# Every fp32r product reads its moving operand and writes its bank from the last column to the first

## The chip, the cores and the metric

One core of a Trainium2 chip. The metric is the device time of one execution, in microseconds; for the kernel before it is 1514.39 us, the median of three runs (1514.04 to 1516.86).

The engines, as the profile names them: PE multiplies matrices, and PEld loads its stationary operands; DVE and ACT work on vectors; POOL and SP here mostly start transfers. A product on PE holds one operand in the array (the stationary one, 128 x 128) and streams the other through it column by column (the moving one, 128 rows by up to 512 columns). Its result lands in a bank of PSUM, 128 partitions by 512 fp32 columns, column by column.

## The reference

Two layers on a sequence of 512 tokens with 1024 features, all in float32. Layer 0 mixes the tokens by windowed attention in three dilated head groups, layer 1 by a gated linear recurrence; each layer ends with a gated feed-forward net with a short convolution.

```python
for layer in range(DEPTH):
    h = rms_norm(x, norm_mix_pre[layer])
    if layer % 2 == 0:
        h = dilated_attention_mixer(h, attn_w_qkv[j], attn_w_o[j], rel_bias)
    else:
        h = rglru_mixer(h, lru_w_in[j], ...)
    x = x + rms_norm(h, norm_mix_post[layer])
    h = rms_norm(x, norm_ffn_pre[layer])
    h = conv_ffn(h, ffn_w_up[layer], ffn_conv_w[layer], ffn_conv_b[layer], ffn_w_down[layer])
    x = x + rms_norm(h, norm_ffn_post[layer])

def conv_ffn(x, w_up, conv_w, conv_b, w_down):
    u = causal_dwconv(x @ w_up, conv_w, conv_b)
    g, v = u[..., :D_FF], u[..., D_FF:]
    return (jax.nn.gelu(g, approximate=True) * v) @ w_down
```

The weights are what is large: 1024 x 9216 for the queries, keys and values, 1024 x 6144 and 3072 x 1024 for each feed-forward net.

## The kernel before

The program holds the activations of all 512 tokens on the chip and streams the weights through. A plan lists the weight chunks in the order of their use; `load` fetches a chunk with one transfer of 1 MB on SP's queue, and `pump` splits it into two fp32r numbers per weight: a high part (`whi`, ACT, line 146) and what is missing (`wlo`, DVE, line 147). The activations are split in the same way (`hT` is a pair of tiles, `ahi` and `alo` are a pair).

A float32 product is then three fp32r products into the same bank, high by high, high by low and low by high. That is the helper `mm3` (lines 237 to 240), and every large product of the kernel goes through it:

- `feat` (lines 348 to 356): features by tokens. The weights are stationary, the normalized activations `hT` are the moving operand, 8 steps over the 1024 input features. A bank `ps` takes 512 tokens in one go, or two halves of 256 (`feat_tiles` with `halves`, at the start of the recurrence and of each feed-forward net). The bank is evacuated by the sinks: `conv` (line 503 on ACT, line 507 on DVE), `qk` (line 580 on ACT, line 582 on DVE; in the dilated groups with the tokens regrouped, which is a read with a step of four columns).
- `values` (bank `v`): tokens by features for the values of the attention. The activations are stationary, 256 columns of weights move; ACT evacuates at line 614.
- `rows_run` (bank `acc`): the output projections. The split activations are stationary, 512 columns of weights move, and up to eight banks are open at once.
- `gates` (bank `gate`): the two gates of the recurrence.

The other matmuls are plain float32 and call `nc.tensor.matmul` or `transpose` directly: the transposes (`tr` line 289, `PT`, `OT`), the scores (`S`, lines 660 and 710) and the weighted values (`O`, lines 695 and 768). Each of these shows as two rows of the profile.

All matmuls stand on PE in the order in which the program is written. Side steps (attention heads, norms) are generators that `tick` advances between tiles. The eight PSUM banks are used in rotation, and the layer that places the tiles adds the waits on semaphores: `PE_49`, `Activation_49` and `DVE_49` count the instructions that each engine has finished.

Of the kernel before, what the change touches and what calls it, by code (L numbers as in the profile page):

```python
# [76 lines left out]
def kernel(  # L77
# [157 lines left out]
        plan.append(("rows", 2, D, [(w[r0 : r0 + 256, :].rearrange("(k p) c -> p k c", p=P), 2)]))  # L235

    def mm3(dst, l, r, start, stop):
        mm(dst, l[0], r[0], start=start, stop=False)  # L238
        mm(dst, l[0], r[1], start=False, stop=False)  # L239
        mm(dst, l[1], r[0], start=False, stop=stop)  # L240
# [107 lines left out]
    def feat(W, hT, dst, n0, n1):  # L348
        for k in range(KD):
            mm3(  # L350
                dst[:, n0:n1],
                [w[:, k, :] for w in W],
                [h[:, k, n0:n1] for h in hT],
                k == 0,
                k == KD - 1,
            )
# [43 lines left out]
    def rows_run(nchunks, A, prep, seq, order, post, pre):  # L400
# [6 lines left out]
        for tiles, chunks in order:  # L407
            for c in chunks:
# [9 lines left out]
                for n, part in enumerate(loop):  # L418
                    prep(seq.index(2 * c + n) + 3)
                    for t, i, kk in part:  # L420
                        k = 2 * c + kk
                        if t not in banks:
                            banks[t] = [psum("acc"), psum("acc")]
                            left[t] = [2 * nchunks, 2 * nchunks]
                        mm3(
                            banks[t][i],
                            [a[:, t * P : (t + 1) * P] for a in A[k]],
                            [v[:, 0, i * 512 : (i + 1) * 512] for v in take(*W[c][kk])],
                            left[t][i] == 2 * nchunks,
                            left[t][i] == 1,  # L430
                        )
                        left[t][i] -= 1
                        uses[k] -= 1
                        if not uses[k]:
                            done()
                    for t in tiles:
                        if left[t] == [0, 0]:
                            side(norms(t, banks[t], post_g, pre_g, hT))
                    tick()
# [94 lines left out]
    def attention(hT, post, pre):  # L534
# [50 lines left out]
        def values(vs, permute):  # L585
# [10 lines left out]
            for tp in range(2):  # L596
                ps = psum("v")
                for t in (2 * tp, 2 * tp + 1):
                    if first_tiles and t < 2:
                        first_tiles[0](t)  # L600
                    W = W or chunk_pair()
                    tok = slice(t * P, (t + 1) * P)
                    for k in range(KD):
                        mm3(
                            ps[:, (t % 2) * 256 : (t % 2) * 256 + 256],
                            [h[:, k, tok] for h in hT],
                            [v[:, k % 4, :] for v in W[k // 4]],
                            k == 0,
                            k == KD - 1,
                        )  # L610
                if first_tiles and not tp:
                    first_tiles[0](2)
                o = gen(s="v")
                nc.scalar.activation(o, ps, AF.Copy)
                if permute:
                    rows = vd[2 * tp * P : (2 * tp + 2) * P, :]
                    nc.sync.dma_start(rows.rearrange("(t p) c -> p t c", p=P), o.rearrange("p (t c) -> p t c", t=2))
                else:
                    vs.append(o)
                if tp:  # L620
                    done(2)
                    if permute:
                        by_residue(vd, vs)
                tick()
# [384 lines left out]
```

## Time and profile before

| what | value |
|---|---|
| median of three runs | 1514.39 us |
| profiled execution | 1513.89 us |
| its span, first to last instruction | 1512.1 us |
| mean granted TensorE clock | 0.994 |
| PE busy, matmuls | 1482.6 us, 7659 rows |
| weight loads busy (PEld) | 1271.1 us |
| DVE / ACT / POOL busy | 798.5 / 631.5 / 53.5 us |
| HBM | 161 MB, 107 GB/s over the span |

A row of the groups reads: line, engine, operation, output tile <- input tiles, array rows x columns, shape and type, count | busy us, mean ns of one | idle us before them, and what ended it. The type of every tile on PE is printed as f32; the fp32r products are those of lines 238 to 240. Matmuls overlap, so the duration of one (389 ns) is longer than the distance to the next; the distance is read from the starts in the timeline. PEld is the weight load that goes with each matmul, and PEldq or PEq is the queue in front of PE.

### The profile page before, as it was taken

The page shows a single profiled execution, that of the slowest core. Times are in us where ns is not written, and L with a number is a line of the kernel's source. Part 1 is how long each engine was busy: PE and PEld are TensorE (multiplying, and loading weights), DVE is VectorE, ACT ScalarE, POOL GpSimd, SP SyncE. Part 2 cuts the span into 40 slices and gives each one's busy share as a digit, 9 for nine tenths or more (in the row PEclk, how much of TensorE's full clock was granted, in tenths as well). Part 3 has the DMA queues.
Part 4 walks back from the last instruction along what each step waited for, and adds up shares of the span by engine and source line. Part 5 has one row for each costly group of instructions (what it writes and reads, how often), then busy time and mean ns, then how long its engine had stood idle before and what let it go on. Part 6 is the DMA issues. An engine that isn't in the chain of part 4 may idle for free.

```text
span 1512.1 us, 19272 instructions
## 1 busy us (share of the span) xinstructions
PE 1482.6 (98%) x7659; PEld 1271.1 (84%) x7659; DVE 798.5 (53%) x1610; ACT 631.5 (42%) x1281; POOL 53.5 (4%) x81
## 2 busy tenths in 40 slices
PE   6999999999999999999999999999899999999997
PEld 5789989898989898888888888988698888888886
DVE  5344334343434586555555336868776555565333
ACT  5243334343333555344344334477554334344321
POOL 3130000000000000000000000003000000000000
PEclk9999999999999999999999999999999999999999
DMA  6642223333333333323233231252224232323301
GB/s 205 211 155 91 65 94 110 105 121 111 109 121 129 98 112 112 111 84 112 84 111 112 84 112 42 71 166 67 96 80 136 84 111 84 109 86 111 112 1 56
DMA packets 120075, 157.72 MB, mean 104 GB/s; under 512 B 4960, under 2 KB 105528, under 8 KB 119985
## 3 DMA queue, kind: packets, MB, share of 16 engines
q1 hardware_dynamic: 115088, 145.24, 29.1%
q0 software_dynamic: 4896, 11.26, 2.2%
q8 instruction: 60, 0.98, 0.3%
q14 instruction: 31, 0.25, 0.1%
HBM read 150.14 MB, written 11.05 MB: 107 GB/s over the span
## 4 chain that ended last, share of the span: by engine, by line
PE 87%; issue 8%; DVE 3%; DMA 1%; POOL 0%; ACT 0%; SPq 0%; DVEq 0%; POOLq 0%
PE ps L238 17%; PE ps L240 17%; PE ps L239 17%; PE acc L240 7%; PE acc L239 7%; PE acc L238 7%; PE v L238 3%; PE v L240 3%; PE v L239 3%; PE O L768 1%; PE S L710 1%; PE O L695 1%; PE tr L289 1%; DVE wlo L147 1%; DMA toe<-skew 1%
## 5 line engine op out<-in xcount | busy, mean ns | idle before, releaser
L238 PE MATMUL ps<-hT,whi 128*128 128x512 f32 (+1 forms) x1376 | 518.6, 377 | 0.0
L240 PE MATMUL ps<-hT,wlo 128*128 128x512 f32 (+1 forms) x1376 | 515.2, 374 | 0.0
L239 PE MATMUL ps<-hT,whi 128*128 128x512 f32 (+1 forms) x1376 | 515.1, 374 | 0.0
L147 DVE TENSOR_TENSOR wlo<-raw,whi 128x512 fp32r<-128x512 f32 x504 | 324.6, 688 | 284.5 <-ACT whi L146 284.3
L146 ACT ACTIVATE whi<-raw 128x512 fp32r<-128x512 f32 x504 | 285.8, 622 | 132.3 <-PE acc L240 120.9
L240 PEld LDWEIGHTS ps<-hT,wlo 128*128 128x128 f32 x1376 | 259.0, 188 | 46.7
L238 PEld LDWEIGHTS ps<-hT,whi 128*128 128x128 f32 x1376 | 259.1, 188 | 46.3 <-issue 0.6
L239 PEld LDWEIGHTS ps<-hT,whi 128*128 128x128 f32 x1376 | 259.2, 188 | 45.8
L507 DVE SCALAR_TENSOR_TENSOR u<-ps,cols,u 128x511 f32<-128x511 f32 x192 | 143.8, 749 | 140.4 <-ACT u L503 137.0
L240 PE MATMUL acc<-whi,alo 128*128 128x512 f32 x512 | 200.4, 391 | 4.2 <-DVE alo L147 4.2
L238 PE MATMUL acc<-whi,ahi 128*128 128x512 f32 x512 | 200.9, 392 | 1.4 <-ACT ahi L146 1.4
L239 PE MATMUL acc<-wlo,ahi 128*128 128x512 f32 x512 | 200.0, 391 | 0.0
L503 ACT ACTIVATE u<-ps,cols 128x512 f32<-128x512 f32 x96 | 74.8, 779 | 209.8 <-PE ps L240 209.8
L240 PEld LDWEIGHTS acc<-whi,alo 128*128 128x128 f32 x512 | 96.7, 189 | 24.6 <-DVE alo L147 4.7
L238 PEld LDWEIGHTS acc<-whi,ahi 128*128 128x128 f32 x512 | 96.7, 189 | 21.7 <-ACT ahi L146 1.8
L239 PEld LDWEIGHTS acc<-wlo,ahi 128*128 128x128 f32 x512 | 96.6, 189 | 20.0
L238 PE MATMUL v<-whi,hT 128*128 128x256 f32 x384 | 111.9, 291 | 0.4 <-ACT hT L293 0.4
L240 PE MATMUL v<-whi,hT 128*128 128x256 f32 x384 | 110.2, 287 | 0.1
L239 PE MATMUL v<-wlo,hT 128*128 128x256 f32 x384 | 109.8, 286 | 0.0
L238 PEld LDWEIGHTS v<-whi,hT 128*128 128x128 f32 x384 | 75.0, 195 | 1.4 <-ACT hT L293 1.1
L240 PEld LDWEIGHTS v<-whi,hT 128*128 128x128 f32 x384 | 74.7, 195 | 0.7 <-DVE hT L294 0.6
L239 PEld LDWEIGHTS v<-wlo,hT 128*128 128x128 f32 x384 | 75.0, 195 | 0.3
(167 smaller groups left out, 1002.3 us busy)
## 6 DMA issues: line engine op xcount, KB each, us to landing
raw<-in_ffn_w_up_dram SPq DMA_DIRECT2D x48, 1024.0 KB, 5.2
raw<-in_attn_w_qkv_dram SPq DMA_DIRECT2D x36, 1024.0 KB, 5.1
raw<-in_ffn_w_down_dram SPq DMA_DIRECT2D x24, 1024.0 KB, 4.8
raw<-in_lru_w_in_dram SPq DMA_DIRECT2D x8, 1024.0 KB, 5.2
skew<-rowv POOLq DMA_DIRECT2D x3, 1536.0 KB, 12.1
vrows<-v SPq DMA_DIRECT2D x16, 256.0 KB, 3.9
vp<-vrows SPq DMA_DIRECT2D x16, 256.0 KB, 3.0
raw<-in_attn_w_o_dram SPq DMA_DIRECT2D x4, 1024.0 KB, 4.8
```

Source lines behind the costliest of these rows:

```text
L146: nc.scalar.activation(hi, raw, AF.Copy)
L147: nc.vector.tensor_tensor(lo, raw, hi.bitcast(F32), op=ALU.subtract)
L238: mm(dst, l[0], r[0], start=start, stop=False)
L239: mm(dst, l[0], r[1], start=False, stop=False)
L240: mm(dst, l[1], r[0], start=False, stop=stop)
L289: nc.tensor.transpose(ps[:, k * P : (k + 1) * P], xs[i][:, k * P : (k + 1) * P], ident)
L503: nc.scalar.activation(u, ps, AF.Identity, scale=cc[:, j : j + 1], bias=cc[:, 48 + j : 49 + j])
L507: nc.vector.scalar_tensor_tensor(u[:, d:], ps[:, : S - d], wc, u[:, d:], op0=ALU.mult, op1=ALU.add)
L695: mm(po[:, a * P : (a + 1) * P], pts[a, j], vtile(v, a - 1 + j, hh), start=j == js[0], stop=j == 1)
L710: mm(ps[:, c], q[hh][:, c], k[hh][:, c], start=True, stop=True)
L768: mm(po[:, c], vtile(qkvs[gi][2], r, hh), pts[gi][:, c], start=gi == 0, stop=gi == 1)
```

## The change

One line in `mm3`: the view of the bank and the two views of the moving operand are turned around in their second dimension before the three products are issued. The stationary operands stay as they are. Column c of the moving operand still lands in column c of the bank, so what is computed is the same; the stream starts at column 511 (or 255) and ends at 0. The plain float32 matmuls keep their direction.

```diff
     def mm3(dst, l, r, start, stop):
+        dst, r = dst[:, ::-1], [v[:, ::-1] for v in r]
         mm(dst, l[0], r[0], start=start, stop=False)
         mm(dst, l[0], r[1], start=False, stop=False)
         mm(dst, l[1], r[0], start=False, stop=stop)
```

In the built program each engine has the same matmuls, vector instructions and transfers in the same order as before (PE 7428 matmuls in both). What differs beside the direction are waits. On PE, 117 matmuls wait on PE's own count that did not before, and 94 of these waits are waiting instructions of their own. In the program of before, a new bank of the first feed-forward net on PE (bank `ps912`, after the last products of `ps908`):

```order
L240 MATMUL ps908_5589<-hT0733_4547,wlo879_5360 128x512
L238 MATMUL ps912_5625<-hT0733_4547,whi883_5397 128x512 [waits Activation_49]
L239 MATMUL ps912_5625<-hT1734_4548,whi883_5397 128x512
L240 MATMUL ps912_5625<-hT0733_4547,wlo884_5398 128x512 [waits DVE_49]
L238 MATMUL ps912_5625<-hT0733_4547,whi883_5397 128x512
```

The same place on PE in the changed program, whose lines stand one lower:

```order
L241 MATMUL ps908_5589<-hT0733_4547,wlo879_5360 128x512
L239 MATMUL ps912_5625<-hT0733_4547,whi883_5397 128x512 [waits PE_49,Activation_49]
L240 MATMUL ps912_5625<-hT1734_4548,whi883_5397 128x512
L241 MATMUL ps912_5625<-hT0733_4547,wlo884_5398 128x512 [waits DVE_49]
L239 MATMUL ps912_5625<-hT0733_4547,whi883_5397 128x512
```

The first product of the bank waits on `PE_49` as well; the values waited for belong to products 41 to 168 matmuls earlier, over all 117.

On DVE, 93 waits on `PE_49` are gone, and 46 waiting instructions with them. At the split of the weights for that same bank, before:

```order
L507 SCALAR_TENSOR_TENSOR u882_5392<-ps881_5367,cols186_1074,u882_5392 128x511 [waits Activation_49]
L507 SCALAR_TENSOR_TENSOR u882_5392<-ps881_5367,cols186_1074,u882_5392 128x510 [waits DVE_49]
L147 TENSOR_TENSOR wlo884_5398<-raw865_5220,whi883_5397 128x512 [waits DMAHW3_49,PE_49,Activation_49]
L147 TENSOR_TENSOR wlo884_5398<-raw865_5220,whi883_5397 128x512 [waits Activation_49]
L507 SCALAR_TENSOR_TENSOR u886_5428<-ps885_5403,cols186_1074,u886_5428 128x511 [waits Activation_49]
```

And in the changed program:

```order
L508 SCALAR_TENSOR_TENSOR u882_5392<-ps881_5367,cols186_1074,u882_5392 128x511 [waits Activation_49]
L508 SCALAR_TENSOR_TENSOR u882_5392<-ps881_5367,cols186_1074,u882_5392 128x510 [waits DVE_49]
L147 TENSOR_TENSOR wlo884_5398<-raw865_5220,whi883_5397 128x512 [waits DMAHW3_49,Activation_49]
L147 TENSOR_TENSOR wlo884_5398<-raw865_5220,whi883_5397 128x512 [waits Activation_49]
L508 SCALAR_TENSOR_TENSOR u886_5428<-ps885_5403,cols186_1074,u886_5428 128x511 [waits Activation_49]
```

The split still waits for ACT's high half and for the transfer; ACT, POOL and SP hold the same rows and waits as before.

## The prediction

> **What bounds the kernel now.** I read the page first: the shares of busy time, then the chain that ended last.
>
> ```profile
> span 1512.1 us, 19272 instructions
> PE 1482.6 (98%) x7659; PEld 1271.1 (84%) x7659; DVE 798.5 (53%) x1610; ACT 631.5 (42%) x1281; POOL 53.5 (4%) x81
> PEclk9999999999999999999999999999999999999999
> PE 87%; issue 8%; DVE 3%; DMA 1%; POOL 0%; ACT 0%; SPq 0%; DVEq 0%; POOLq 0%
> ```
>
> PE is busy for 1482.6 of 1512.1 us, its granted clock stands in the top tenth in every slice, and 87% of the chain that set the end is PE. PE sits idle for 1512.1 - 1482.6 = 29.5 us in all. So whatever the change does to the time of a matmul comes out at the end, nearly one for one, and whatever it does to another engine does not.
>
> A busy time of pipelined matmuls does not say what one costs, so next I read the timeline of PE, once where the products are 512 columns wide and once where they are 256 wide.
>
> ```profile
> 1375.88 0.39 PE L238 MATMUL acc<-whi,ahi 128*128 128x512 f32 x1
> 1376.10 0.39 PE L239 MATMUL acc<-wlo,ahi 128*128 128x512 f32 x1
> 1376.33 0.39 PE L240 MATMUL acc<-whi,alo 128*128 128x512 f32 x1
> 1376.56 0.39 PE L238 MATMUL acc<-whi,ahi 128*128 128x512 f32 x1
> ```
> ```profile
> 559.91 0.28 PE L238 MATMUL ps<-hT,whi 128*128 128x256 f32 x1
> 560.03 0.28 PE L239 MATMUL ps<-hT,whi 128*128 128x256 f32 x1
> 560.15 0.28 PE L240 MATMUL ps<-hT,wlo 128*128 128x256 f32 x1
> 560.27 0.28 PE L238 MATMUL ps<-hT,whi 128*128 128x256 f32 x1
> ```
>
> The reader is to look at the starts, not the durations. Three products of 512 columns take 1376.56 - 1375.88 = 0.68 us, so one starts every 227 ns. Three of 256 columns take 0.36 us, one every 120 ns. The difference of 107 ns over 256 columns is 0.418 ns a column, and what is left, 120 - 107 = 13 ns, is the same for both widths: a fixed price of each product, in which no column moves.
>
> Then the groups by shape, for how many products there are.
>
> ```profile
> L238 PE MATMUL ps<-hT,whi 128*128 128x512 f32 x1184 | 463.8, 392 | 0.0
> L240 PE MATMUL ps<-hT,wlo 128*128 128x512 f32 x1184 | 461.0, 389 | 0.0
> L239 PE MATMUL ps<-hT,whi 128*128 128x512 f32 x1184 | 460.8, 389 | 0.0
> L238 PE MATMUL acc<-whi,ahi 128*128 128x512 f32 x512 | 200.9, 392 | 1.4 <-ACT ahi L146 1.4
> L240 PE MATMUL acc<-whi,alo 128*128 128x512 f32 x512 | 200.4, 391 | 4.2 <-DVE alo L147 4.2
> L239 PE MATMUL acc<-wlo,ahi 128*128 128x512 f32 x512 | 200.0, 391 | 0.0
> L238 PE MATMUL v<-whi,hT 128*128 128x256 f32 x384 | 111.9, 291 | 0.4 <-ACT hT L293 0.4
> L240 PE MATMUL v<-whi,hT 128*128 128x256 f32 x384 | 110.2, 287 | 0.1
> L239 PE MATMUL v<-wlo,hT 128*128 128x256 f32 x384 | 109.8, 286 | 0.0
> L238 PE MATMUL ps<-hT,whi 128*128 128x256 f32 x192 | 54.8, 285 | 0.0
> L239 PE MATMUL ps<-hT,whi 128*128 128x256 f32 x192 | 54.3, 283 | 0.0
> L240 PE MATMUL ps<-hT,wlo 128*128 128x256 f32 x192 | 54.3, 283 | 0.0
> L238 PE MATMUL gate<-xhi,whi 128*128 128x512 f32 x32 | 12.4, 389 | 0.0
> L239 PE MATMUL gate<-xlo,whi 128*128 128x512 f32 x32 | 12.4, 389 | 0.0
> L240 PE MATMUL gate<-xhi,wlo 128*128 128x512 f32 x32 | 12.4, 389 | 0.0
> ```
>
> These are all the products that `mm3` issues, and all that the change touches. Of 512 columns there are 3 x (1184 + 512 + 32) = 5184, of 256 columns 3 x (384 + 192) = 1728: 6912 products. At 227 and 120 ns that is 1177 + 207 = 1384 us, 92% of the span. In columns it is 5184 x 512 + 1728 x 256 = 3,096,576, and at 0.418 ns each 1294 us is the pure streaming of columns.
>
> **The change, part by part.** It adds and removes no product, changes no shape and moves no instruction. It has two parts with a price: the direction of the streams, and waits.
>
> *The direction.* Each of 6912 products now reads 512 or 256 fp32r columns downward from SBUF, and writes the bank downward. The trace holds no matmul whose operand or output steps by anything but one column upward, so the price is bounded from both sides. The lower end is nothing: the same columns, the same bank, one after the other. Below nothing there is no room that I can name: 0.418 ns a column is the fastest column in this trace, and a direction takes no part in the fixed 13 ns as far as rows show. The upper end comes from the nearest rows in which PE takes its columns slower, the plain f32 products of the attention scores:
>
> ```profile
> L660 PE MATMUL S<-qk,qk 128*128 128x256 f32 x48 | 11.7, 380 | 0.0
> L660 PE MATMUL S<-qk,qk 128*128 128x128 f32 x16 | 3.1, 273 | 0.0
> ```
>
> 128 columns more take 380 - 273 = 107 ns, 0.836 ns a column: twice the price of an fp32r column. fp32r thus takes two columns where these rows take one. If its double rate rests on taking neighbouring columns in rising order as a pair, a falling order loses it, and each column costs 0.836 - 0.418 = 0.418 ns more: 3,096,576 x 0.418 = 1294 us.
>
> Which end is nearer? The trace shows other engines on access patterns with steps. ACT evacuates the score operands' bank at line 580 in plain order before 205 us, and with a step of four columns between 215 and 490 us; line 774 is the one write with a step of four columns, and line 614 is a plain evacuation to set beside it.
>
> ```profile
> L580 ACT ACTIVATE qk<-ps 128x512 f32<-128x512 f32 x10 | 6.0, 596 | 32.4 <-PE ps L240 28.4 <-PE cols L459 4.0
> L580 ACT ACTIVATE qk<-ps 128x512 f32<-128x512 f32 x14 | 8.4, 599 | 59.1 <-PE ps L240 35.5 <-issue 23.6
> L774 ACT ACTIVATE oT<-O 128x512 f32<-128x512 f32 x8 | 8.8, 1097 | 41.8 <-PE O L768 38.3 <-issue 3.5
> L614 ACT ACTIVATE v<-v 128x512 f32<-128x512 f32 x24 | 14.2, 591 | 79.1 <-PE v L240 79.1
> ```
>
> Reading the bank with a step costs ACT nothing (596 against 599 ns); writing SBUF 16 bytes apart costs it 1097 / 591 = 1.86 times. So a pattern's step can double a transfer, but the doubling row is one in which neighbours in time lie 16 bytes apart. Reversed columns lie 4 bytes apart, as near as before, which is the case of the rows without a price. I take nothing as the value, and keep 1294 us as the other end.
>
> Two pages bear on this, and they point in opposite directions. The Trainium skill, "Advanced Engine Details and Errata", section Memory Cachelines, counts how many accesses in a row fall on one line of 16 bytes in SBUF. Line 774 agrees with that (one element a line, 1.86 times), and by that rule a reversed run, four elements a line, stays at 0.418 ns and the time at 1514 us. The Trainium skill, "PSUM — Partial Sum Buffer", section Specifications (TRN2), says that any non-contiguous access pattern slows matmuls significantly. Read strictly, a run with step -1 is such a pattern, and the time would be that of the halved rate below; no row here shows a matmul with such an output.
>
> *The waits.* The changed program asks PE for 117 waits on PE's own earlier products that were not asked before; 94 of them come as a waiting instruction of their own ahead of the matmul (first product of a bank, mostly in the feature tiles of the two FFNs). Behind each stands the whole PE queue. The product waited for lies 41 to 168 products back, at 120 ns or more each at least 41 x 120 ns = 4.9 us, so it has long ended: the wait finds its value there. What is left is the instruction itself. Its kind is in the profile of before:
>
> ```profile
> L238 PEldq EVENT_SEMAPHORE  x41: 51/51/51, 33.6 to 1376.5; - x41
> ```
>
> 51 ns each, if nothing hid it: 94 x 51 ns = 4.8 us, 0.3%. The last of them began at 1376.5, and the timeline quoted above shows the products around it 220 to 230 ns apart, as everywhere: the queue had taken it ahead of time. I take nothing, with 4.8 us as the upper end; if the queue ran dry the cover would be gone.
>
> On DVE 93 waits on PE fall away, at the low halves of the weight splits (line 147). DVE is busy for 53% of the span, and the products waited for line 147 for 4.2 us in the groups above; I take nothing for it, and 4 us of gain at most. POOL, SP and the DMA queues hold the same rows as before.
>
> *Sum.* The profiled execution took 1513.89 us, its span and 1.8 us around it; the median of three runs is 1514.39. With nothing added and nothing taken the forecast is the median, 1514.4 us, and its own range is 1510 (the 4 us from DVE) to 1519 (the 4.8 us of the waits).
>
> **The rivals.** *The falling order loses the double rate* (slower). Its place is every product of `mm3`; it decides as soon as the pairing looks for rising neighbours, on the read or on the write. For it: fp32r is exactly twice as fast as f32 here, which says that something is taken two at a time, and the 1.86 times of line 774. Against it: reversed pairs stay within the same neighbourhood, and the stepped reads of line 580 are free. Price: 1513.9 + 1294 = 2808 us, less at most the 29.5 us of idle time that a slower PE would cover: 2779 to 2808, with line 774's 1.86 in place of 2 it is 1513.9 + 0.86 x 1294 = 2627. I take 2800 us.
>
> *A fixed price per product*: the stream starts at the end of a line, and each product pays something once, between nothing and its present fixed part again, 6912 x 13 ns = 90 us; the exposed 4.8 us of waits are of this kind too. For it: a fixed part exists. Against: it is the same at both widths, so it looks like the change of weights and not like the stream. 1518 to 1604 us.
>
> *A worse loss than the double rate*: each column alone, at twice the f32 price, 4 x 0.418 ns: 1513.9 + 3 x 1294 = 5396 us. No row shows such a rate on PE.
>
> *Faster*: only by the DVE waits that fall away, at most 4 us, 1510. That the two reversals are undone when the program is made into instructions gives the forecast's time.
>
> **How the numbers follow.** The forecast 0.50; the lost double rate 0.32; a fixed price 0.10; the worse loss 0.05; faster 0.03. A measurement of this kernel tells about 0.2%, 3 us, from no change; the forecast stands for "within 0.2%", and the three slower cases together for slower, 0.47. The predicted time is that of the likeliest case. The forecast and the fixed price hold only 0.60, so the range has to reach the lost double rate: 1510 to 2830 us, the last 22 us for a fixed price on top; it leaves out the worse loss and part of the faster case.
>
> **What would show it.** Right: starts of 512-wide products still 227 ns apart and of 256-wide ones 120, durations 389 to 392 and 283 to 291 ns, PE idle near 30 us, the new waits in the rows of PE's queue with the cadence around them unbroken. The lost double rate: starts about 441 and 227 ns apart, so 0.836 ns a column, with the plain f32 rows at 380 and 273 ns as they are, and idle shares of DVE and ACT up. A fixed price: both widths longer by the same number of ns. I am wrong if the starts differ from 227 by more than 1 ns.

## The result, and the profile after

The changed kernel takes 1542.61 us, the median of five runs (1540.88 to 1543.44), against 1514.39 us before: ratio 1.0182, 95% interval 1.0168 to 1.0196, 28 us slower. The forecast was no change. That the time lies in the stated range is luck: the range reached that far for a much larger loss by another mechanism. What happened is nearest to the rival with a fixed price per product, and differs from it in one point that turned out to be the key: the two widths did not change alike.

The page of the changed kernel, the same rows as before:

```profile
span 1540.8 us, 19320 instructions
...
PE 1513.6 (98%) x7659; PEld 1270.4 (82%) x7659; DVE 798.7 (52%) x1610; ACT 631.4 (41%) x1281; POOL 53.2 (3%) x81
...
PEclk9999999999999999999999999999999999999999
...
PE 87%; issue 8%; DVE 3%; DMA 1%; ACT 0%; POOL 0%; DVEq 0%; SPq 0%; POOLq 0%
```

The span grew by 28.7 us; PE's busy time grew by 31.0 us and its idle time shrank by 2.3. No other engine's busy time moved by more than 0.7 us. The clock is as before, and PE's share of the chain that ended last is 87% in both. The 48 instructions more are 94 waits more on PE and 46 fewer on DVE. So the loss lies inside the products, and the timeline shows it in the output projection (512 columns) and in the half banks (256 columns):

```profile
1404.32 0.40 PE L239 MATMUL acc<-whi,ahi 128*128 128x512 f32 x1
1404.55 0.40 PE L240 MATMUL acc<-wlo,ahi 128*128 128x512 f32 x1
1404.79 0.40 PE L241 MATMUL acc<-whi,alo 128*128 128x512 f32 x1
1405.02 0.40 PE L239 MATMUL acc<-whi,ahi 128*128 128x512 f32 x1
...
1405.72 0.40 PE L239 MATMUL acc<-whi,ahi 128*128 128x512 f32 x1
```
```profile
570.06 0.28 PE L239 MATMUL ps<-hT,whi 128*128 128x256 f32 x1
570.18 0.28 PE L240 MATMUL ps<-hT,whi 128*128 128x256 f32 x1
570.30 0.28 PE L241 MATMUL ps<-hT,wlo 128*128 128x256 f32 x1
...
571.48 0.28 PE L239 MATMUL ps<-hT,whi 128*128 128x256 f32 x1
```

Six wide products take 1405.72 - 1404.32 = 1.40 us, 233.3 ns each where it was 226.7. Twelve narrow ones take 571.48 - 570.06 = 1.42 us, 118.3 ns each where it was 120. The wide ones got dearer by 6.7 ns, the narrow ones cheaper by 1.7. The prediction had named starts more than 1 ns off 227 as the sign that it is wrong. The groups by shape show the same for the wide products, which last 8 ns longer (400 and 397 against 392 and 389 ns); a narrow one lasts as long as before, and so does a plain f32 product (`S`, 380 ns), which was not turned around.

```profile
L239 PE MATMUL ps<-hT,whi 128*128 128x512 f32 x1184 | 473.3, 400 | 0.0
L240 PE MATMUL ps<-hT,whi 128*128 128x512 f32 x1184 | 470.5, 397 | 0.0
...
L239 PE MATMUL v<-whi,hT 128*128 128x256 f32 x384 | 111.9, 291 | 0.0
...
L661 PE MATMUL S<-qk,qk 128*128 128x256 f32 x48 | 11.7, 380 | 0.0
```

Summed over the distances between starts in the two traces, the wide products take 31.1 us more (22.4 in `ps`, 8.1 in `acc`, 0.6 in `gate`), the narrow ones 2.2 us less, and everything else 0.1 us less: 28.7 us, the whole difference of the spans.

### The profile page after: what moved, and what is told of

It reads as the page before. It is cut to its first block, busy times and chain, and to the rows that moved or that the text cites. A ratio compares the mean times of both kernels' runs of the same rounds, so it can differ in the third digit from the quotient of the medians.

```text
span 1540.8 us, 19320 instructions
## 1 busy us (share of the span) xinstructions
PE 1513.6 (98%) x7659; PEld 1270.4 (82%) x7659; DVE 798.7 (52%) x1610; ACT 631.4 (41%) x1281; POOL 53.2 (3%) x81
## 4 chain that ended last, share of the span: by engine, by line
PE 87%; issue 8%; DVE 3%; DMA 1%; ACT 0%; POOL 0%; DVEq 0%; SPq 0%; POOLq 0%
PE ps L239 17%; PE ps L241 17%; PE ps L240 17%; PE acc L241 7%; PE acc L240 7%; PE acc L239 7%; PE v L239 3%; PE v L241 3%; PE v L240 3%; PE O L769 1%; PE S L711 1%; PE O L696 1%; PE tr L290 1%; DVE wlo L147 1%; DMA toe<-skew 1%
## 5 line engine op out<-in xcount | busy, mean ns | idle before, releaser
L239 PE MATMUL ps<-hT,whi 128*128 128x512 f32 (+1 forms) x1376 | 527.9, 384 | 0.0
L240 PE MATMUL ps<-hT,whi 128*128 128x512 f32 (+1 forms) x1376 | 524.6, 381 | 0.0
L241 PE MATMUL ps<-hT,wlo 128*128 128x512 f32 (+1 forms) x1376 | 524.5, 381 | 0.0
L241 PE MATMUL acc<-whi,alo 128*128 128x512 f32 x512 | 204.2, 399 | 4.2 <-DVE alo L147 4.2
L239 PE MATMUL acc<-whi,ahi 128*128 128x512 f32 x512 | 204.8, 400 | 0.1
L240 PE MATMUL acc<-wlo,ahi 128*128 128x512 f32 x512 | 204.1, 399 | 0.0
```

## The experiments

Theory one: the downward order of the *read* of the moving operand has a price. Theory two: the downward *write* of the bank has it. Later a third came up: it is not the direction at all, but how the read of the moving operand meets, in SBUF, the load of the next product's weights that runs under it. The waits were the rival from the prediction. Distances of starts given below without a fence are means over the second half of a row of equal products in that run's trace.

### One side alone

```diff
-        dst, r = dst[:, ::-1], [v[:, ::-1] for v in r]
+        r = [v[:, ::-1] for v in r]
```

> Only the moving operand is read downward; the bank is written upward, so every product lands mirrored in its bank (the output is not the reference's). If the price sits in the downward read: 512-wide products start 233 ns apart as in the changed kernel, about 1543 us. If it sits in the downward write: 227 ns and about 1514 us. If it needs both (the two streams against each other): neither, 227 ns and 1514 us. If it were the added waits: 1514 to 1519 us with starts of 227 ns between the waits.

Measured: 1541.62 us, ratio to before 1.0181 (1.0162 to 1.0200).

```diff
-        dst, r = dst[:, ::-1], [v[:, ::-1] for v in r]
+        dst = dst[:, ::-1]
```

> Only the bank is written downward; the moving operand is read upward, so every product lands mirrored (the output is not the reference's). If the price sits in the downward write: 512-wide starts 233 ns apart, about 1543 us. If in the read: 227 ns, about 1514 us. If each direction costs something: e1 and this one between 1514 and 1543 us and adding up to the 28 us.

Measured: 1513.76 us, ratio 0.9998 (0.9989 to 1.0007). The groups of the first and of the second, one row each for the wide products:

```profile
L239 PE MATMUL ps<-hT,whi 128*128 128x512 f32 x1184 | 473.3, 400 | 0.0
```
```profile
L239 PE MATMUL ps<-hT,whi 128*128 128x512 f32 x1184 | 463.8, 392 | 0.0
```

The read carries the whole price, the write none. The same pair settles the waits. Only the kernel that writes downward has the added waits (the one that reads downward has as many waiting instructions as the kernel before), and PE's queue shows most of them at the first product of `mm3`:

```profile
L239 PEldq EVENT_SEMAPHORE  x117: 51/51/51, 32.9 to 1375.2; - x117
```

At this line there were 41 waiting instructions of 51 ns each before and there are 117 now, 76 more; over all of PE's queue the traces count 99 and 193, which are the 94 more of the change. (That 117 is also the number of added waits is chance.) The kernel is not slower, so the 94 were taken under running products.

### The narrow products alone

```diff
-        dst, r = dst[:, ::-1], [v[:, ::-1] for v in r]
+        if dst.shape[1] == 256:
+            dst, r = dst[:, ::-1], [v[:, ::-1] for v in r]
```

> Only the 256-wide products (values and half banks) are turned around, both in read and write. If the profile of the changed kernel is right that only 512-wide products got dearer: 1514 us or up to 2 us less, since 1694 starts of 256-wide products were 1 ns closer on average. If the price is a fixed one per product: 1728 x 6.7 ns = 12 us more, 1526 us. If it is the waits: about 5 us more at most.

Measured: 1511.20 us, ratio 0.9981 (0.9972 to 0.9990): 2.6 us faster, as the 118.3 ns said. A fixed price per product is out: the same edit costs a product of 512 columns 6.7 ns and gives one of 256 columns 1.7.

### Rows of products by width and direction

A kernel that only does this, in the place of the trunk:

```python
def run(name, cols, read, write, count=96, flip=None):
    ps = psum(name)
    for n in range(count):
        k = n // 3
        l = wt[(2 * k + (n % 3 == 2)) % 16]
        r = mv[(k + (n % 3 == 1)) % 4]
        f, g = flip if flip and n % 2 else (read, write)
        mm(g(ps[:, :cols]), l, f(r[:, :cols]), start=n == 0, stop=n == count - 1)
    ...
```

> No part of the reference: 96 fp32r products in a row into one bank, with a new stationary operand each (repeated as in the three-product helper), for seven widths from 512 to 128, upward and downward, then read and write direction apart at 512 and 256, alternating directions, and 512 columns in blocks of 2, 4, 8 and 256 whose order is reversed while each block runs upward. A price per column of the downward stream: the extra grows with the width, 6.7 ns at 512 and 3.3 ns at 256. A price per product that the narrow products hide behind something else (the weight load): nothing up to a width, then about 6.7 ns for all wider ones. A pairing or line rule: blocks of 2 or of 4 cost as little as upward. A rule on the start of the stream: blocks of 256 cost as much as downward.

| columns | 512 | 448 | 384 | 320 | 256 | 192 | 128 |
|---|---|---|---|---|---|---|---|
| upward, ns from start to start | 226.7 | 202.7 | 173.3 | 146.7 | 120.0 | 111.7 | 111.6 |
| downward, ns | 233.3 | 206.8 | 177.8 | 146.7 | 118.2 | 111.6 | 111.6 |

No stage of the trunk is needed: products in a row show 226.7 and 233.3 ns by themselves. In the groups of this kernel (busy is here the length of the whole row of 96 products) the rows at 512 columns are:

```profile
L163 PE MATMUL rdown<-mv,wt 128*128 128x512 f32 x96 | 22.6, 398 | 0.0
L163 PE MATMUL rev<-mv,wt 128*128 128x512 f32 x96 | 22.6, 397 | 0.0
...
L163 PE MATMUL quads<-mv,wt 128*128 128x512 f32 x96 | 22.6, 397 | 0.0
...
L163 PE MATMUL serp<-mv,wt 128*128 128x512 f32 x96 | 22.3, 393 | 0.0
L163 PE MATMUL wdown<-mv,wt 128*128 128x512 f32 x96 | 21.9, 389 | 0.0
L163 PE MATMUL halfs<-mv,wt 128*128 128x512 f32 x96 | 21.9, 389 | 0.0
```

Read downward (`rdown`) costs, written downward (`wdown`) does not; rows of alternating directions (`serp`) lie in the middle (229.9 ns). Two things fit no price of the direction: blocks of 2, 4 (`quads`) or 8 columns from last to first cost as much as single columns (233.3 ns) although they are read upward inside, and two blocks of 256 in reversed order (`halfs`) cost nothing (226.7 ns) although the stream starts in the middle. The growth with the width is no straight line either: 0 at 320, 4 to 4.5 at 384 and 448, 6.7 at 512.

### Where the two operands lie

```diff
...
+            if wat:
+                l = wide[:, (k + (n % 3 == 2)) % 4, wat : wat + P]
...
-            r = mv[(k + (n % 3 == 1)) % 4]
+            m = (k + (n % 3 == 1)) % 4
+            r = mv[m] if at is None else wide[:, m, at : at + cols]
```

> No part of the reference: 512-wide fp32r products in a row as in the run on widths, reading upward or downward. Theory one, the price belongs to the read of the moving operand alone: 226.7 ns upward and 233.3 ns downward whatever the stationary operand is and wherever both lie. Theory two, the fixed 13.3 ns and its growth to 20 ns are the meeting of two reads of SBUF, the stream of the moving operand and the weight load of the next product under it: then the numbers move with the place of the moving operand or of the weights (other offsets in their tiles), with the same weights loaded again and again, and above all with weights that lie 2 or 4 columns apart, which the load fetches from 2 or 4 times as many places: upward up to 240 and 267 ns, if 128 weights in a row cost the stream 13.3 ns. Reversed blocks: the price is there for blocks of 8 (233 ns) and gone for blocks of 256; the width at which it goes says over how many columns the downward order has to run.

Upward at 512 columns, by the place of the moving operand against the weights in SBUF: 226.7 ns at 0, 64, 128 and 256 columns, but 236.7 at 1, 233.3 at 2, 231.6 at 4, 233.3 at 8, 228.9 at 16 and 232.2 at 32. Moving the weights does the same: 233.3 to 233.4 at 4 and 16, 232.4 at 32, 226.7 at 64 and 128. Downward it is 233.3 to 236.7 at all these places. Weights that lie 2 or 4 columns apart give 233.3 and 234.9 ns upward, more than side by side, but far from the 240 and 267 that I had expected if each place fetched cost the same; loading one and the same weights each time changes nothing (226.7 and 233.3). Reversed blocks cost up to 32 columns (232.2 ns) and cost nothing from 64 on (226.7). Four rows of this run's page: the moving operand 1 column on (`upatb`), weights 4 columns apart with their load (`wfourup`), and the weights 4 columns on (`wupa`):

```profile
L171 PE MATMUL upatb<-wide,wt 128*128 128x512 f32 x96 | 22.9, 399 | 0.0
...
L171 PE MATMUL wfourup<-mv,wide 128*128 128x512 f32 x96 | 22.7, 398 | 0.0
L171 PEld LDWEIGHTS wfourup<-mv,wide 128*128 128x128 f32 x96 | 22.6, 310 | 0.0
...
L171 PE MATMUL wupa<-mv,wide 128*128 128x512 f32 x96 | 22.6, 396 | 0.0
```

So theory one falls as it stood. An upward read costs as much as a downward one, or more, when its operand lies elsewhere against the weights, and places 64, 128 and 256 columns on are like place 0; 64 fp32 columns are 256 bytes. That it matters where the weights lie points to their load as one side of it. The length of the load does not set the price: with weights 4 columns apart a load lasts 310 ns in place of 188, and downward products still start every 233.3 ns.

> No part of the reference: rows of 60 fp32r products, 512 and then 256 columns wide, with the moving operand 0, 4, 8 ... 60 columns further into its tile than the weights (counted within 64 columns, 256 bytes), upward and downward. If the price is the direction alone: two numbers per width, one for each direction, whatever the place. If it is the meeting of the two reads, as the run on places says: 512 wide 226.7 ns upward only where both lie alike, 229 to 237 ns elsewhere, and downward 233 to 237 ns; were the downward order only another meeting, some place downward should come down to 227 ns. 256 wide: 120 and 118.3 ns where both lie alike; no guess elsewhere, a place under 118 ns would be a way to a faster kernel.

| moving operand, columns on from the weights | 0 | 4 | 8 | 12 | 16 | 20 | 24 | 28 | 32 | 36 | 40 | 44 | 48 | 52 | 56 | 60 |
|---|---|---|---|---|---|---|---|---|---|---|---|---|---|---|---|---|
| 512 wide, upward, ns | 226.7 | 231.8 | 233.3 | 233.4 | 228.9 | 231.1 | 233.2 | 231.3 | 233.5 | 233.3 | 234.4 | 233.2 | 233.3 | 234.5 | 233.4 | 233.3 |
| 256 wide, upward, ns | 120.0 | 118.6 | 116.7 | 118.3 | 113.3 | 120.1 | 119.8 | 113.3 | 118.7 | 118.6 | 117.3 | 119.5 | 117.8 | 119.3 | 118.5 | 117.1 |

Places 8 (`upc`), 16 (`upe`) and 0 (`upa`) in the groups, rows of 60:

```profile
L171 PE MATMUL upc<-wide,wt 128*128 128x512 f32 x60 | 14.2, 395 | 0.0
...
L171 PE MATMUL upa<-wide,wt 128*128 128x512 f32 x60 | 13.8, 389 | 0.0
...
L171 PE MATMUL upa<-wide,wt 128*128 128x256 f32 x60 | 7.4, 283 | 0.0
...
L171 PE MATMUL upe<-wide,wt 128*128 128x256 f32 x60 | 7.0, 276 | 0.0
```

Downward, 512 columns stay at 233.2 to 233.5 ns at every place (236.6 at 60), 256 columns between 117.8 and 120.1. My expectation that some place would bring the downward read down to 227 ns did not come true, so the downward order is not just another place. Upward, place 0, whose 226.7 and 120.0 ns are those of the kernel, is the best of the sixteen for the wide products, and close to the worst for the narrow ones.

### The same loss without turning anything around

The kernel before, with 32 unused bytes ahead of its weight tiles:

```diff
+    ap = ctx.enter_context(tc.tile_pool(name="ap", bufs=1))
+    ap.tile([P, 8], F32, tag="apart", name="apart")
     wp = ctx.enter_context(tc.tile_pool(name="wp", bufs=W_UNITS))
```

> The kernel before, all reads upward, with one unused piece of 8 fp32 columns (32 bytes) placed ahead of the weight tiles, so that weights and work tiles lie 8 columns further against the normalized activations than before. If the price is the meeting of the weight load with the stream, no reversal is needed for it: by the run on offsets the 512-wide products of the feature tiles (activations moving, 56 columns on) go to 233.4 ns, 3552 x 6.7 = 24 us; the half banks to 118.5 and the values (8 columns on) to 116.7 ns, 5 us less; the output projections, whose two operands shift together, stay at 227 ns: about 1533 us. If the price is the direction: no change, 1514 us.

Measured: 1530.95 us (1529.47 to 1531.98), ratio 1.0113 (1.0096 to 1.0129). The groups:

```profile
L240 PE MATMUL ps<-hT,whi 128*128 128x512 f32 x1184 | 471.1, 398 | 0.0
...
L241 PE MATMUL ps<-hT,whi 128*128 128x512 f32 x1184 | 468.2, 395 | 0.0
L240 PE MATMUL acc<-whi,ahi 128*128 128x512 f32 x512 | 200.6, 392 | 0.4 <-ACT ahi L148 0.4
...
L240 PE MATMUL v<-whi,hT 128*128 128x256 f32 x384 | 110.2, 287 | 0.0
```

The feature tiles, whose operands now lie apart, last 6 ns longer and start 233 ns apart; the output projections, whose operands moved together, stay at 392 and 227 ns; the values are a little cheaper. All reads are upward. Over the starts of the two traces the wide feature products take 22.2 us more, where the change cost the same products 22.4 us: a loss of the same size, from the place alone.

### Reversed in blocks of 64

```diff
-        dst, r = dst[:, ::-1], [v[:, ::-1] for v in r]
+        def turned(v):
+            return v.rearrange("p (b c) -> p b c", c=64)[:, ::-1, :]
+
+        dst, r = turned(dst), [turned(v) for v in r]
```

> The change with its order reversed only between blocks of 64 columns, upward inside each, read and write alike; the result is the reference's. If what costs is the order inside 64 columns (256 bytes), 512-wide starts are back at 227 ns: 1514 us. If what costs is that the stream starts at the far end of the operand or of the bank: 233 ns and 1543 us.

Measured: 1514.29 us, ratio 1.0006 (0.9997 to 1.0015). A reversal of whole stretches of 256 bytes is free in the kernel, too.

### Other orders, and a faster kernel

> No part of the reference: rows of 60 fp32r products, 256 and then 512 columns wide, both operands at like places, read and written in other orders: blocks of 2 to 64 columns from the last to the first, upward inside, and blocks from the first to the last, downward inside. If it is the meeting of two reads within 64 columns: blocks of 2 to 16 backward like downward (118 and 233 ns), of 64 like upward (120 and 227 ns); downward inside 2, 4 or 8 columns like upward, inside 64 like downward. Were it the step of -1 as such, every order that is downward inside would cost 233 ns at 512 columns. An order with less than 118 ns at 256 columns would be a faster kernel.

Rows of 96 were run rather than 60. Groups at 512 and 256 columns, with "back" for reversed blocks that run upward inside and "turn" for blocks in order that run downward inside:

```profile
L177 PE MATMUL turnsixteen<-mv,wt 128*128 128x512 f32 x96 | 25.8, 432 | 0.0
...
L177 PE MATMUL down<-mv,wt 128*128 128x512 f32 x96 | 22.6, 397 | 0.0
...
L177 PE MATMUL up<-mv,wt 128*128 128x512 f32 x96 | 21.9, 389 | 0.0
...
L177 PE MATMUL turntwo<-mv,wt 128*128 128x512 f32 x96 | 21.9, 389 | 0.0
L177 PE MATMUL turnfour<-mv,wt 128*128 128x512 f32 x96 | 21.9, 389 | 0.0
...
L177 PE MATMUL up<-mv,wt 128*128 128x256 f32 x96 | 11.7, 283 | 0.0
...
L177 PE MATMUL down<-mv,wt 128*128 128x256 f32 x96 | 11.5, 282 | 0.0
...
L177 PE MATMUL turneight<-mv,wt 128*128 128x256 f32 x96 | 11.1, 276 | 0.0
```

Downward inside 2 or 4 columns is as fast as upward (226.7 ns): a step of -1 has no price of its own. Downward inside 16 is far worse (266.7 ns, and 133.3 at 256 columns), downward inside 32 takes 240.0 ns; no price of a direction gives that. Two guesses were off: blocks of 8 backward at 256 columns cost 120.0 and not 118 ns, and downward inside 8 is not like upward, but 233.3 ns at 512 columns and, at 256, the best of all orders: 113.3 ns. That one was put into the kernel for its narrow products:

```diff
-        dst, r = dst[:, ::-1], [v[:, ::-1] for v in r]
+        def turned(v):
+            return v.rearrange("p (b c) -> p b c", c=8)[:, :, ::-1]
+
+        if dst.shape[1] == 256:
+            dst, r = turned(dst), [turned(v) for v in r]
```

> Only the 256-wide products are changed: both read and write go through blocks of 8 columns from the first to the last, downward inside each. The 512-wide products stay upward. By the run on orders a 256-wide product then starts every 113.3 ns in place of 120: 1694 starts x 6.7 ns = 11 us less, about 1503 us, where the 256-wide products downward throughout gave 2.5 us. If in the kernel the weight load or the other traffic hides it: 1511 to 1514 us.

Measured: 1506.72 us (1506.06 to 1508.58), ratio 0.9955 (0.9941 to 0.9968), faster than both kernels by 7 and 36 us. The half banks start 113 to 114 ns apart nearly throughout; of the 1127 starts among the values 468 stayed at 120 ns, about 3 us of the 11 expected, and the wait of the weighted values for DVE grew by 1.0 us. The 468 fall on whole banks: in 10 of the 24 banks of values nearly every start is at 120 ns, in the other 14 few are. What sets those ten apart was not tried and stays open.

## Why the prediction failed

**The reading of the bound held.** PE's products were the bound and nearly all of their change came out at the end: 31.1 - 2.2 = 28.9 us of products made 28.7 us of span.

**The value taken for the direction failed.** The prediction bounded it by nothing and 1294 us and took nothing, because reversed columns are "the case of the rows without a price"; those were rows of ACT. It measured 31.1 us on 5184 wide products (6.7 ns each in a steady row, 6.0 on average) and -2.2 us on 1728 narrow ones. The two ends were both prices per column, and the price is not one per column. The step that broke is that the lower end was nothing, because "a direction takes no part in the fixed 13 ns as far as rows show". The fixed 13 ns were read as a constant of the product, "the same for both widths". That sameness was no evidence: a price per column and a rest, worked out from two widths, fit both by construction. The sixteen places show that the rest is not constant: 226.7 to 234.5 ns upward at 512 columns, and 113.3 to 120.1 at 256, with the same number of columns streamed.

**"Below nothing there is no room that I can name" failed** in the same way: the narrow products got 1.7 ns faster.

**The rule on non-contiguous patterns.** The Trainium skill, "PSUM — Partial Sum Buffer", section Specifications (TRN2), would have made a downward output slow; the run that only writes downward is at 0.9998. A bank written with step -1 does not act as such a pattern here, and neither does one written in blocks of 64, at 1.0006.

**The rule on lines of 16 bytes** (the Trainium skill, "Advanced Engine Details and Errata", section Memory Cachelines) pointed to the forecast. As far as it goes these runs agree: there was no halving, and downward inside 4 columns, which are 16 bytes, is free (226.7 ns). But blocks of 4 columns from last to first cost 233.3 ns with the same four accesses in a row, so this price is another one.

**The lost double rate and the worse loss** did not occur: 233.3 and 118.2 ns downward leave no room for 0.836 ns a column.

**The fixed price** had the size right, 1518 to 1604 us, and the mechanism wrong: it wanted the same addition at both widths.

**The waits** were costed rightly at nothing: 94 more waiting instructions of 51 ns left the kernel that only writes downward where it was. So were the waits that DVE lost: that kernel has lost them too (241 waiting instructions on DVE where there were 287), and gained nothing.

What takes the place of the failed step, as far as shown: the extra time of a product comes from the read of the moving operand, and it depends on the order of its columns within 256 bytes and, in upward order above all, on where that operand lies against the weights within 256 bytes; a loss of the same size can be had upward by 32 bytes of displacement. That the other party is the load of the next product's weights under the running stream is argued from this dependence on the place; a product without a weight load was not run, nor one whose weights are read in another direction. That the downward order and the displacement cost the same collision is argued too, from the equal size (233.3 ns in both). What within 256 bytes collides, why the downward order stays near 233 ns at nearly every place, and why downward inside 16 columns is the worst, stays open. The Trainium skill, "TensorE: Matmul & The Clock Gate", section Step-by-step: what each phase is for, says that loading the next tile's weights doesn't steal SBUF read bandwidth from the running matmul. For fp32r products these runs speak against it: with the moving operand in place, weights 4 columns on take the product from 226.7 to 233.4 ns. Where the two differ, the measurement decides.

## What to carry to other kernels

When a row of matmuls takes some nanoseconds more than its columns account for, vary where moving operand and weights lie in SBUF against each other before calling that rest a constant: here 32 bytes made 1.1% of the kernel, and the layout of the kernel before had given the wide products the best place tried and the narrow ones a poor one. Whether that was chance isn't on record: the kernel before has an unused piece of 8 columns of its own (`pad`, line 110) ahead of the tiles of its first pool. Measure it by a row of 96 bare products per placement, one run for dozens of them, and at each width apart, since what suits one width costs another. And when an unknown price is bounded by rows of another engine or another rate, keep a third case between the ends: small, of either sign, and in the part that was taken for constant.

## What the runs showed of the hardware

- In steady rows of fp32r products with a weight load each, 128 and 192 columns both start every 111.6 ns. At 256 columns the least that any order or place gave is 113.3 ns, not the 120 of this kernel.
- At 512 columns no order and no placement tried went under 226.7 ns; the worst, downward inside blocks of 16, took 266.7 ns, 18% more, for the same columns.
- In a row of products whose every second one is read downward the distances alternate between 227 and 233 ns (mean 229.9), so the price belongs to the single product and not to a change of direction.
